# A hybrid encoder block: the first MLP product turned token-major, two of its eight K pairs by a seven-product scheme

## The chip, the cores and the metric

The kernel runs on one core of one Trainium2 chip. The metric is the device time of one execution in microseconds, as the median of the runs. The engines are called PE (TensorE), ACT (ScalarE), DVE (VectorE), POOL (GpSimd) and SP (SyncE, which here only issues DMA transfers). Each works through its own row of instructions in order.

## The reference

One layer over 256 tokens of width 2048, all in float32:

```python
n = rms_norm(h, norm_mix_w)                 # h = x
y = token_mixer(n @ w_in)                   # 8 gated DeltaNet heads, 8 HGRN2 heads, chunked recurrences
h = h + y @ w_out                           # 2048 x 2048
n = rms_norm(h, norm_ffn_w)
h = h + square(relu(n @ w_ff1)) @ w_ff2     # 2048 -> 8192 -> 2048
out = rms_norm(h, norm_final_w)
```

The change concerns `n @ w_ff1`: 256 tokens, K = 2048, 8192 columns out.

## The kernel before

Every large product is done as three products of float32r numbers. `split` (L111) makes them: ACT casts a block to float32r (`hi`, L117), DVE subtracts that from the block (`lo`, L118), and the product is hi*hi + hi*lo + lo*hi, summed in PSUM. Weights come in tiles of 1 MB (`wtile`, 128 x 2048, three buffers, loaded on SP's queue), and each is split in two halves of 128 x 1024, into a pool `spool` of three pairs of buffers. The activations are split once and stay in SBUF.

The stages, in the order of the program:

1. The input projection (L270 to L295) and the head mixers. Projections of the next head are issued among the mixing of the one before. The last two HGRN2 heads (`hgrn_mix`, L518 to L619) are long chains of small steps on DVE, ACT, POOL and PE: gates (L527 to L543), a scan (L547), decay factors `E` (L553 to L569), small matmuls `pd` and `pa` (L583 to L598), a masked sum (L601 to L608), copies (L611 to L615), the output `poh` (L617, L618) and `finish_heads` (L386): a square, its split, two matmuls `pm` (L398, L399), the scaling, and at last the split of the head's output into `yTb` (L117, L118). All tiles of the mixer lie in the pool `mp`, which is closed after the last head (`mctx.close()`, L636).
2. W_out (L652 to L671), two halves of 1024 columns, 192 matmuls each; then h is added, squared and summed, and 16 blocks of h are transposed on PE (L678) and split into `hT` (`to_T`), with the norm's weight; its row scale is applied at the very end, since the squared ReLU lets it pass.
3. The first MLP product (L698 to L715), feature-major: the weight block of 128 x 128 is stationary and the tokens move. For each K block and each of four blocks of features there are two matmuls: L709 with `hi` against both parts of the tokens (512 columns) and L710 with `lo` against the high part (256). After K, ACT copies and DVE adds the two halves of the bank, and DVE makes the squared ReLU. The result `g` is already as the second product needs it.
4. The second MLP product (L735 to L756), token-major: `gs`, the split of a block of g, is stationary, and the weights move, 512 columns at a time, three matmuls for each bank (L731).
5. The last norm and the output.

PSUM has four banks `acc` (psA) and, once the mixer is closed, four banks `accb` (psB).

The instructions are not put in the order in which the code is written: a scheduler lays out each engine's row when the program is built, so W_out's matmuls stand among those of the last heads. A tile of a pool that takes over the memory of a closed pool waits until the old pool's instructions are done.

Of the kernel before, what the change touches and what calls it, by code (L numbers as in the profile page):

```python
# [7 lines left out]
F32 = mybir.dt.float32  # L8
F32R = mybir.dt.float32r
AF = mybir.ActivationFunctionType  # L10
ALU = mybir.AluOpType
# [4 lines left out]
P = 128  # L16
T = 256
D = 2048
KT = D // P
DFF = 8192  # L20
NH = 8
CH = 64
EPS = 1e-6
LEVELS = (32, 16, 8, 4, 2)
NL = len(LEVELS)
NM = NL + 1
# [47 lines left out]
def hybrid_block(ctx: ExitStack, tc: tile.TileContext, x, xt, w_in, w_ab, params, w_out, w_ff1, w_ff2,  # L74
                 norm_final_w, consts, out):
    nc = tc.nc
    PE, ACT, DVE, POOL, SP = nc.tensor, nc.scalar, nc.vector, nc.gpsimd, nc.sync
# [11 lines left out]
    psA = ctx.enter_context(tc.tile_pool(name="psA", bufs=4, space=PSUM))  # L89

    yctx = ExitStack()
    ypool = yctx.enter_context(tc.tile_pool(name="ypool", bufs=1))
    NYA = 12
    yTa = ypool.tile([P, NYA, 2 * T], F32R, tag="yT", name="yTa")
# [7 lines left out]
    def acc_a():  # L102
        return psA.tile([P, 512], F32, tag="acc", name="acc")
# [19 lines left out]
        return hi, lo  # L123


    big = bpool.tile([P, 2 * D], F32, tag="h", name="big")
    x3 = big.rearrange("p (k t) -> p k t", k=KT)
    cst = cpool.tile([P, consts.shape[1]], F32, tag="cst", name="cst")
# [12 lines left out]
    for a, b in zip(xs, ws):  # L141
        SP.dma_start(*a)
        SP.dma_start(*b)
    SP.dma_start(cst, consts)
    wab = mp.tile([P, KT, 16], F32, tag="Xt", name="wab")
    SP.dma_start(wab, w_ab)

    def C(name):
        a, b = _CONST_COLS[name]
        return cst[:, a:b]  # L150

    ident, ones = C("ident"), C("ones")
    eps = C("eps")
# [487 lines left out]
    def acc_b():  # L641
        return psB.tile([P, 512], F32, tag="accb", name="accb")

    hT = bpool.tile([P, KT, 2 * T], F32R, tag="xT", name="hT")
    h = bpool.tile([P, 2 * D], F32, tag="h", name="h").rearrange("p (f c) -> p f c", f=2)
# [5 lines left out]
    fs = cpool.tile([P, 16], F32, tag="fs", name="fs")  # L651
    for nh in range(2):  # L652
        accs = [acc_a() for _ in range(4)]
        for kp in range(8):
            w = wtile()
            SP.dma_start(w, w_out[nh * 8 + kp])
            for kk in range(2):
                k = 2 * kp + kk
                hi, lo = split(w[:, kk * 1024:(kk + 1) * 1024], 1024)
                for hf in range(2):  # L660
                    for a, ww in ((0, hi), (T, hi), (0, lo)):
                        st = yT(k, a + hf * P, a + hf * P + P)
                        for c in range(2):
                            PE.matmul(accs[2 * hf + c], lhsT=st, rhs=ww[:, c * 512:(c + 1) * 512],  # L664
                                      start=(k == 0 and a == 0 and ww is hi), stop=(k == 2 * NH - 1 and ww is lo))
        for hf in range(2):
            for c in range(2):
                hv = h[:, hf, nh * 1024 + c * 512:nh * 1024 + (c + 1) * 512]
                DVE.tensor_tensor(out=hv, in0=accs[2 * hf + c], in1=hv, op=ALU.add)
            hv = h[:, hf, nh * 1024:(nh + 1) * 1024]  # L670
            ACT.activation(sqj, hv, AF.Square, accum_out=fs[:, 2 * hf + nh:2 * hf + nh + 1])  # L671
        for k2 in range(4):
            pt = acc_b()
            for kk in range(2):
                k = nh * 8 + k2 * 2 + kk
                ptk = pt[:, kk * T:(kk + 1) * T]
                for hf in range(2):
                    PE.transpose(ptk[:, hf * P:(hf + 1) * P], h[:, hf, k * P:(k + 1) * P], ident)  # L678
                to_T(hT, k, ptk, cols[:, 16 + k:17 + k])
    for hf in range(2):  # L680
        DVE.tensor_tensor(out=fs[:, 4 + hf:5 + hf], in0=fs[:, 2 * hf:2 * hf + 1], in1=fs[:, 2 * hf + 1:2 * hf + 2],
                          op=ALU.add)
    DVE.tensor_scalar(fs[:, 4:6], fs[:, 4:6], 1.0 / D, EPS, ALU.mult, ALU.add)
    DVE.reciprocal(fs[:, 6:8], fs[:, 4:6])
    octx.close()
    yctx.close()


    fp = ctx.enter_context(tc.tile_pool(name="fp", bufs=1))
    NF = DFF // P  # L690
    NG = NF // 2
    gt = [fp.tile([P, NG, T], F32, tag=f"g{i}", name=f"g{i}") for i in range(2)]

    def g(f):
        return gt[f // NG][:, f % NG, :]

    nfw = fp.tile([P, D], F32, tag="nfw", name="nfw")
    for fg in range(NF // 4):  # L698
        accs = [acc_a() if fg % 2 == 0 else acc_b() for _ in range(4)]
        for kq in range(4):  # L700
            w = wtile()
            SP.dma_start(w, w_ff1[fg * 4 + kq])
            for q in range(2):
                hi, lo = split(w[:, q * 1024:(q + 1) * 1024], 1024)
                for kk in range(2):
                    k = 4 * kq + 2 * q + kk
                    for f in range(4):
                        cs = slice(kk * 512 + f * P, kk * 512 + (f + 1) * P)
                        PE.matmul(accs[f], lhsT=hi[:, cs], rhs=hT[:, k, :], start=(k == 0), stop=False)  # L709
                        PE.matmul(accs[f][:, T:], lhsT=lo[:, cs], rhs=hT[:, k, 0:T], start=False, stop=(k == KT - 1))  # L710
# [7 lines left out]
    accs = [[acc_a() for _ in range(4)], [acc_b() for _ in range(4)]]  # L718
    TAIL = 3
    held = []  # L720

# [10 lines left out]
                      start=(first and a == 0 and ww is hi), stop=(last and ww is lo))  # L732

    keep = None
    for f in range(NF):  # L735
        w = wtile()
        SP.dma_start(w, w_ff2[f])
        gs = fp.tile([P, 2 * T], F32R, tag="gs", name="gs", bufs=4)
        split(g(f), None, gs[:, 0:T], gs[:, T:])
        n = f - (NF - TAIL)  # L740
        if n == 0:
            keep = fp.tile([P, TAIL - 1, 2, D], F32R, tag="g0", name="keep")
        hl = []
        for q in range(2):
            qs = slice(q * 1024, (q + 1) * 1024)
            if 0 <= n < TAIL - 1:
                hl.append(split(w[:, qs], None, keep[:, n, 0, qs], keep[:, n, 1, qs]))
            else:
                hl.append(split(w[:, qs], 1024))
# [7 lines left out]
    fin = fp.tile([P, 12], F32, tag="fin", name="fin")  # L757
    sqf = fp.tile([P, 512], F32, tag="sqf", name="sqf")
    o = fp.tile([P, 2, D], F32, tag="o", name="o", bufs=1)
    NP = 5  # L760
    DVE.memset(fin, 0.0)

    def piece(hf, n, a, b, acc):
        hv = h[:, hf, a:b]
        DVE.scalar_tensor_tensor(out=hv, in0=acc, scalar=fs[:, 6 + hf:7 + hf], in1=hv, op0=ALU.mult, op1=ALU.add)
        ACT.activation(sqf[:, 0:b - a], hv, AF.Square, accum_out=fin[:, hf * NP + n:hf * NP + n + 1])
        DVE.scalar_tensor_tensor(out=o[:, hf, a:b], in0=hv, scalar=float(D) ** 0.5, in1=nfw[:, a:b], op0=ALU.mult,
                                 op1=ALU.mult)

    def row_rstd(hf, n, last):  # L770
# [11 lines left out]

    def scaled(hf, eng, a, b, s):
        if eng is ACT:
            ACT.activation(h[:, hf, a:b], o[:, hf, a:b], AF.Copy, scale=s)
        else:
            DVE.tensor_scalar(h[:, hf, a:b], o[:, hf, a:b], s, None, ALU.mult)
        (ACT if eng is ACT else SP).dma_start(out[0, hf * P:(hf + 1) * P, a:b], h[:, hf, a:b])

    hv = h[:, 1, 1536:2048]  # L790
# [10 lines left out]
            ff2(f, 1, c, gs, hl)  # L801
        piece(1, c, c * 512, (c + 1) * 512, accs[1][c])
    for n in range(2):
        bank = acc_a()[:, 0:256]
# [13 lines left out]
def _laid_out(i):  # L818
# [5 lines left out]
    for base in (0, 4112):  # L824
        v = w[:, base:base + 4096].reshape(2, 8, P, 2, 2, NH, P)
        groups.append(v.transpose(5, 3, 0, 2, 1, 4, 6).reshape(4 * NH, P, 2048))

    def columns(a):
        return a.reshape(-1, P).T

# [9 lines left out]
        "w_ff1": i["w_ff1"][0].reshape(4, 4, P, 16, 512).transpose(3, 0, 2, 1, 4).reshape(64, P, 2048),  # L840
# [24 lines left out]
```

## Time and profile before

| | us |
|---|---|
| median of three runs | 1272.61 (1271.04 to 1273.03) |
| the profiled execution | 1271.04 |
| its span, from the first instruction to the last | 1269.3 |
| PE busy (matmuls) | 1239.6 |
| DVE, ACT, POOL busy | 855.0, 673.9, 166.3 |
| mean granted clock of TensorE | 0.994 of full |

A row of the profile's timeline gives the start, the duration, the engine, the line of the kernel, the operation, output<-inputs, the shape, and how many instructions are merged in the row; in brackets stands how long the engine had been idle and what released it. Matmuls overlap one another: the distance between two starts tells the pace, not the duration. In a row of a table by stretches of time there are, after the stretch and its length, the busy time of PE, PE's weight loads, DVE, ACT and POOL, each with the number of instructions, then the granted clock, the share of DMA and GB/s. In a group row the numbers are count | busy us, mean ns of one | idle time before.

### The profile page before, as it was taken

To read this page: it belongs to the slowest core of one execution; us is meant where nothing else is said; L and a number is where in the kernel's file an instruction comes from. 1 tells how busy PE (TensorE), PEld (TensorE's weight loads), DVE (VectorE), ACT (ScalarE), POOL (GpSimd) and SP (SyncE) were. 2 spreads that over 40 slices of the span, in tenths; PEclk is the share of its full clock that TensorE was granted. 3 is DMA by queue.
4 is the path that set the end of the run, shared out by engine and by line. 5 is a ranking of instruction groups with operands and counts; after the bars stand their busy time and mean duration, and the time that the engine had idled before them with its cause. 6 is when DMAs were issued, how large, how long until landed. Compare 5 with 4: busy or idle time off the path is not lost.

```text
span 1269.3 us, 18524 instructions
## 1 busy us (share of the span) xinstructions
PE 1239.6 (98%) x7293; PEld 1050.3 (83%) x7293; DVE 855.0 (67%) x1211; ACT 673.9 (53%) x973; POOL 166.3 (13%) x216
## 2 busy tenths in 40 slices
PE   7999999998999999999999999999999999999997
PEld 5888888876788887888888888888888888888886
DVE  7789999889988996566555565555655545545556
ACT  7567677655667775455444444444444444444453
POOL 1233433278300130000000000000000000000000
PEclk9999999998999999999999999999999999999999
DMA  8455555533434544465555545555455555555552
GB/s 314 147 176 172 179 186 187 173 141 133 151 104 174 189 167 166 168 222 177 197 181 184 199 170 195 189 178 196 168 201 195 199 199 190 187 191 195 199 201 97
DMA packets 35798, 229.65 MB, mean 181 GB/s; under 512 B 4536, under 2 KB 5440, under 8 KB 8960
## 3 DMA queue, kind: packets, MB, share of 16 engines
q1 hardware_dynamic: 33408, 225.63, 50.4%
q0 software_dynamic: 1728, 2.11, 1.3%
q8 instruction: 57, 0.93, 0.3%
q10 hardware_dynamic: 576, 0.74, 0.2%
q14 instruction: 29, 0.24, 0.1%
HBM read 225.83 MB, written 2.63 MB: 180 GB/s over the span
## 4 chain that ended last, share of the span: by engine, by line
issue 62%; PE 30%; POOL 3%; DVE 2%; DMA 2%; ACT 0%; SPq 0%; POOLq 0%; ACTq 0%; DVEq 0%
PE acc L286 15%; PE acc L287 8%; PE acc L664 3%; POOL Xt L424 1%; POOL X L426 1%; DMA big<-in_xt_dram 1%; DMA w<-in_w_in_dram 1%; DVE E L568 1%; PE pk L368 1%; DVE E L553 0%; DVE lo L118 0%; PE pd L583 0%; PE pab L221 0%; PE po L507 0%; PE pk L369 0%
## 5 line engine op out<-in xcount | busy, mean ns | idle before, releaser
L118 DVE TENSOR_TENSOR lo<-w,hi 128x1024 fp32r<-128x1024 f32 (+1 forms) x416 | 517.3, 1244 | 363.5 <-ACT hi L117 362.4
L117 ACT CAST hi<-w 128x1024 fp32r<-128x1024 f32 (+1 forms) x416 | 433.2, 1042 | 442.0 <-PE accb L731 177.1
L286 PE MATMUL acc<-xT,hi 128*128 128x512 f32 x1024 | 363.3, 401 | 7.1 <-ACT hi L117 6.7
L287 PE MATMUL acc<-xT,lo 128*128 128x256 f32 x1024 | 283.9, 286 | 6.2 <-DVE lo L118 6.2
L286 PEld LDWEIGHTS acc<-xT,hi 128*128 128x128 f32 x1024 | 191.6, 191 | 47.3 <-ACT hi L117 7.3
L287 PEld LDWEIGHTS acc<-xT,lo 128*128 128x128 f32 x1024 | 194.9, 191 | 15.0 <-DVE lo L118 10.5
L709 PE MATMUL acc<-hT,hi 128*128 128x512 f32 x512 | 181.3, 399 | 0.0
L709 PE MATMUL accb<-hT,hi 128*128 128x512 f32 x512 | 180.8, 398 | 0.0
L731 PE MATMUL accb<-hi,gs 128*128 128x512 f32 x494 | 170.0, 389 | 0.0
L710 PE MATMUL accb<-hT,lo 128*128 128x256 f32 x512 | 143.2, 281 | 0.0
L710 PE MATMUL acc<-hT,lo 128*128 128x256 f32 x512 | 142.8, 281 | 0.0
L731 PE MATMUL acc<-hi,gs 128*128 128x512 f32 (+1 forms) x500 | 134.2, 388 | 0.0
L709 PEld LDWEIGHTS accb<-hT,hi 128*128 128x128 f32 x512 | 96.1, 188 | 23.9
L709 PEld LDWEIGHTS acc<-hT,hi 128*128 128x128 f32 x512 | 96.0, 188 | 23.4
L731 PEld LDWEIGHTS acc<-hi,gs 128*128 128x128 f32 x500 | 93.7, 188 | 19.3
L731 PEld LDWEIGHTS accb<-hi,gs 128*128 128x128 f32 x494 | 92.7, 188 | 19.3
L779 POOL TENSOR_TENSOR fin<-fin,cst 128x1 f32<-128x1 f32 x2 | 1.1, 564 | 773.9 <-issue 766.5
L710 PEld LDWEIGHTS acc<-hT,lo 128*128 128x128 f32 x512 | 96.5, 189 | 0.2
L710 PEld LDWEIGHTS accb<-hT,lo 128*128 128x128 f32 x512 | 96.6, 189 | 0.1
L731 PE MATMUL accb<-lo,gs 128*128 128x512 f32 x247 | 95.4, 389 | 0.0
L731 PE MATMUL acc<-lo,gs 128*128 128x512 f32 (+1 forms) x250 | 77.7, 388 | 0.0
L731 PEld LDWEIGHTS acc<-lo,gs 128*128 128x128 f32 x250 | 46.9, 188 | 9.7
(251 smaller groups left out, 1250.1 us busy)
## 6 DMA issues: line engine op xcount, KB each, us to landing
w<-in_w_ff_dram SPq DMA_DIRECT2D x128, 1024.0 KB, 4.9
w<-in_w_in_dram SPq DMA_DIRECT2D x62, 1024.0 KB, 4.9
w<-in_w_out_dram SPq DMA_DIRECT2D x16, 1024.0 KB, 4.9
big<-in_xt_dram SPq DMA_DIRECT2D x8, 256.0 KB, 6.2
w<-in_w_in_dram SPq DMA_DIRECT2D x8, 256.0 KB, 6.3
h<-in_x_dram SPq DMA_DIRECT2D x2, 1024.0 KB, 9.2
dt<-scr_g POOLq DMA_DIRECT2D x8, 128.0 KB, 5.6
nfw<-in_norm_final_w_dram SPq DMA_DIRECT2D x1, 1024.0 KB, 4.7
```

The source lines that it names most:

```text
L117: ACT.copy(hi, w)
L118: eng.tensor_tensor(out=lo, in0=w, in1=hi.bitcast(F32), op=ALU.subtract)
L286: PE.matmul(accs[g], lhsT=hi[:, kk, g, :], rhs=xT[:, k, :], start=(k == 0), stop=False)
L287: PE.matmul(accs[g][:, T:], lhsT=lo[:, kk, g, :], rhs=xT[:, k, 0:T], start=False, stop=(k == KT - 1))
L368: PE.matmul(pk0, lhsT=R[:, 1, 0:P], rhs=qk.rearrange("p a t -> p (a t)"), start=True, stop=True)
L424: POOL.tensor_tensor(out=t3, in0=X[:, j, j + 1:].unsqueeze(2).to_broadcast([np_, nr, ncol]), in1=X[:, j, 0:ncol].unsqueeze(1).to_broadcast ...
L426: POOL.tensor_tensor(out=X[:, j + 1:, 0:ncol], in0=X[:, j + 1:, 0:ncol], in1=t3, op=ALU.subtract)
L568: DVE.tensor_tensor(out=ev, in0=ev, in1=view(gx, 0, [[2 * m, nb], [T + m, 2], [1, m]]), op=ALU.mult)
L664: PE.matmul(accs[2 * hf + c], lhsT=st, rhs=ww[:, c * 512:(c + 1) * 512], start=(k == 0 and a == 0 and ww is hi), stop=(k == 2 * NH - 1 and ...
L709: PE.matmul(accs[f], lhsT=hi[:, cs], rhs=hT[:, k, :], start=(k == 0), stop=False)
L710: PE.matmul(accs[f][:, T:], lhsT=lo[:, cs], rhs=hT[:, k, 0:T], start=False, stop=(k == KT - 1))
L731: PE.matmul(dst, lhsT=gs[:, a + hf * P:a + hf * P + P], rhs=ww[:, at:at + n], start=(first and a == 0 and ww is hi), stop=(last and ww is lo))
```

## The change

*The first product becomes token-major*, as the second is: a block of 128 tokens (high or low part) is stationary, and 512 columns of weights move (`product`, three matmuls). The 8192 columns are done in 8 groups (`ng`) of 1024, two blocks of 512; four banks E hold the two token halves by the two column blocks. K goes in 8 pairs (`kp`) of two blocks of 128. Six pairs are plain: 24 matmuls each.

*Pairs 2 and 5 (`SUMS`) use the Strassen-Winograd scheme*: seven products of sums of token blocks with sums of weight blocks, in place of eight, 21 matmuls. The token sums are formed and split once (`blocks`, `a_sums`). The weight sums are formed on DVE for each tile (`TT`: one difference of 1024 columns, two of 512), and three pairs and a half of hi and lo are split in place of two. Four of the products go to four more banks M; after pair 5 they are combined into `C4` (a copy on ACT, four additions on DVE), and at the end of the group the E banks are added to that (four additions on DVE) and ACT applies the ReLU. E and M are the banks acc and accb by turns.

*The result is token-major and has to be turned*: `turn` transposes four blocks of 128 x 128 on PE and ACT squares the bank into g. The turns of a group are kept in a list, `fills`, and issued two at a time in the next group, so their banks are E's of the group before. The 16 transposes of h go into the same list for the second half.

*Buffers.* A second pool of split buffers, `wp2`, has two pairs; `split_pair` takes pairs 1, 2 and 5 of each five from `spool` and pairs 3 and 4 from `wp2`, from W_out on. `wp2` and `tp` (`TT`, a half pair and the second set of token sums) are opened at the right end of SBUF after the mixer is closed. h is written to DRAM in four pieces of 512 KB and loaded back (with the final norm's weight) after the first product, on SP's queue. The constants that only the mixer needs move into `mp`. The first two blocks of the second product do their first 1024 columns ahead of their second.

The core of the diff:

```diff
+    wp2 = ctx.enter_context(tc.tile_pool(name="wp2", bufs=2, side="right"))
+    t1 = ExitStack()
+    tp = t1.enter_context(tc.tile_pool(name="tp", bufs=1, side="right"))
+    pairs = [0]
+    def split_pair(w):
+        n = pairs[0] = pairs[0] + 1
+        pool, t = (spool, "") if n % 5 < 3 else (wp2, "2")
+        return split(w, None, *[pool.tile([P, 1024], F32R, tag=p + t, name=p + t) for p in ("hi", "lo")])
...
     for nh in range(2):
-        accs = [acc_a() for _ in range(4)]
+        acc = (acc_a, acc_b)[nh]
+        accs = [acc() for _ in range(4)]
...
-                hi, lo = split(w[:, kk * 1024:(kk + 1) * 1024], 1024)
+                hi, lo = split_pair(w[:, kk * 1024:(kk + 1) * 1024])
...
+            SP.dma_start(scr_h[hf, :, nh * 1024:(nh + 1) * 1024], hv)
...
+    def product(dst, a, b, start, stop):
+        (ah, al), (bh, bl) = a, b
+        PE.matmul(dst, lhsT=ah, rhs=bh, start=start, stop=False)
+        PE.matmul(dst, lhsT=al, rhs=bh, start=False, stop=False)
+        PE.matmul(dst, lhsT=ah, rhs=bl, start=False, stop=stop)
+    def turn(ng, n, src, acc):
+        half, hf = n // 2, n % 2
+        pt = acc()
+        for c in range(4):
+            PE.transpose(pt[:, c * P:(c + 1) * P], src[:, c * P:(c + 1) * P], ident)
+        ACT.activation(g(8 * ng + 4 * half, 4)[:, :, hf * P:(hf + 1) * P], pt.rearrange("p (c t) -> p c t", c=4),
+                       AF.Square)
...
-                    for f in range(4):
-                        cs = slice(kk * 512 + f * P, kk * 512 + (f + 1) * P)
-                        PE.matmul(accs[f], lhsT=hi[:, cs], rhs=hT[:, k, :], start=(k == 0), stop=False)
-                        PE.matmul(accs[f][:, T:], lhsT=lo[:, cs], rhs=hT[:, k, 0:T], start=False, stop=(k == KT - 1))
-        for f in range(4):
-            lot = fp.tile([P, T], F32, tag="lotf", name="lotf", bufs=2)
-            ACT.copy(lot, accs[f][:, T:])
-            DVE.tensor_tensor(out=lot, in0=accs[f][:, 0:T], in1=lot, op=ALU.add)
-            DVE.scalar_tensor_tensor(out=g(4 * fg + f), in0=lot, scalar=0.0, in1=lot, op0=ALU.max, op1=ALU.mult)
+    for ng in range(NGR):
+        bank_e, bank_m = (acc_a, acc_b) if ng % 2 == 0 else (acc_b, acc_a)
+        E = [bank_e() for _ in range(4)]
+        M = None
+        for kp in range(KP):
+            w = wtile()
+            SP.dma_start(w, w_ff1[ng * KP + kp])
+            if kp not in SUMS:
+                B12, B11 = halves(split_pair(w[:, 0:1024]))
+                B21, B22 = halves(split_pair(w[:, 1024:2048]))
+                plain_quad(E, a_plain(kp), ((B11, B12), (B21, B22)), kp == 0, kp == KP - 1, 0 if kp == 0 else 2)
+                if kp == 0:
+                    fill(2)
...
+            for dst, a, b in ((E[0], 1, B21), (E[1], 6, B22), (p5, 3, B1), (p7, 5, B3), (p6, 4, B2), (E[2], 2, B4),
+                              (p1, 0, B11)):
+                m = a in (0, 3, 4, 5)
+                product(dst, A[a], b, a0 and m, z0 and m)
...
+        for at, p in ((0, E[0]), (2, E[1]), (1, E[2]), (3, E[3])):
+            DVE.tensor_tensor(out=C4[:, at], in0=p, in1=C4[:, at], op=ALU.add)
+            ACT.activation(C4[:, at], C4[:, at], AF.Relu)
+            fills.append(lambda ng=ng, at=at, src=C4[:, at], acc=bank_e: turn(ng, at, src, acc))
```

What the scheduler makes of it, at three places. Lines ahead of the change move by four (L399 becomes L403, L617 becomes L621), and W_out's matmul L664 becomes L726.

PE's row around the last HGRN2 head, before (`pvh` is that head's first matmul, `pd` and `pa` follow; `acc<-hi` and `acc<-lo` are W_out's):

```order
L664 MATMUL acc<-lo,yTa 128x512 x4
L664 MATMUL acc<-hi,yTa 128x512
L522 MATMUL pvh<-cst,R 128x128 x2
L664 MATMUL acc<-hi,yTa 128x512 x2
L583 MATMUL pd<-E 32x32 x32
L586 MATMUL pd<-gx 32x64 x8
L592 MATMUL pa<-E 32x32 x4
L596 MATMUL pa<-E 64x64 x2
L598 MATMUL pa<-L 128x128
L664 MATMUL acc<-hi,yTa 128x512
L664 MATMUL acc<-lo,yTa 128x512 x2
L664 MATMUL acc<-hi,yTa 128x512 x4
```

The same head in PE's row after the change, to its end:

```order
L526 MATMUL pvh<-cst,R 128x128 x2
L587 MATMUL pd<-E 32x32 x8
L596 MATMUL pa<-E 32x32 x4
L587 MATMUL pd<-E 32x32 x24
L590 MATMUL pd<-gx 32x64 x8
L600 MATMUL pa<-E 64x64 x2
L602 MATMUL pa<-L 128x128
L621 MATMUL poh<-A,vv 128x256
L622 MATMUL poh<-A,vv 128x128
L402 MATMUL pm<-shi,ones_r 128x256
L403 MATMUL pm<-slo,ones_r 128x256
L726 MATMUL acc<-hi_5066,yTa 128x512 x8
```

Of W_out's 384 matmuls, 180 stand ahead of the last head's L399 before, and 24 ahead of its L403 after. `hi_5066` is the third pair of W_out, the first from `wp2`.

ACT's row at the end of the same head, before:

```order
L117 CAST hi<-w 128x1024 x2
L392 ACTIVATE fsq<-poh 128x256
L396 CAST shi<-fsq 128x256
L117 CAST hi<-w 128x1024 x2
L400 ACTIVATE fsq<-pm,cst 128x256
L401 ACTIVATE fsq<-fsq 128x256
L117 CAST yTb<-fsq 128x256
L117 CAST hi<-w 128x1024
```

And after:

```order
L619 COPY A<-pa 32x2x32 x2
L396 ACTIVATE fsq<-poh 128x256
L400 CAST shi<-fsq 128x256
L404 ACTIVATE fsq<-pm,cst 128x256
L405 ACTIVATE fsq<-fsq 128x256
L119 CAST yTb<-fsq 128x256
L119 CAST hi_5066<-w 128x1024
L119 CAST hi_5082<-w 128x1024
```

The casts of W_out's weights that stood between the head's steps are gone from there, and the third and fourth pair (`hi_5066`, `hi_5082`) come behind its last cast.

DVE's row at the end of a group of the first product, before (four blocks of features) and after (1024 columns; `C` is C4, the four additions of L835 to L838 are those of the M banks):

```order
L118 TENSOR_TENSOR lo<-w,hi 128x1024 x7
L714 TENSOR_TENSOR lotf<-acc,lotf 128x256 x2
L715 SCALAR_TENSOR_TENSOR g_5658<-lotf 128x256 x2
L118 TENSOR_TENSOR lo<-w,hi 128x1024
L714 TENSOR_TENSOR lotf<-acc,lotf 128x256 x2
```

```order
L838 TENSOR_TENSOR C_7937<-accb,C_7937 128x512
L120 TENSOR_TENSOR lo<-w,hi 128x1024
L816 TENSOR_TENSOR TT<-w 128x1024
L120 TENSOR_TENSOR lo_8138<-w,hi_8137 128x512
L120 TENSOR_TENSOR lo<-w,hi 128x1024
L841 TENSOR_TENSOR C_7937<-acc,C_7937 128x512
L819 TENSOR_TENSOR TT<-w,TT 128x512
L841 TENSOR_TENSOR C_7937<-acc,C_7937 128x512 x2
L820 TENSOR_TENSOR TT<-w,TT 128x512
L841 TENSOR_TENSOR C_7937<-acc,C_7937 128x512
L120 TENSOR_TENSOR lo<-w,hi 128x1024
```

Ahead of the E additions (L841) stand a split and the first difference for the next group; the additions come among the next two differences (L819, L820), and more splits behind them.

More of the change, by code (lines that the diff above doesn't have):

```diff
@@ L23 @@
 EPS = 1e-6
+NKEEP = 130
 LEVELS = (32, 16, 8, 4, 2)
@@ L149, in C @@
         a, b = _CONST_COLS[name]
-        return cst[:, a:b]
+        return cst[:, a:b] if b <= NKEEP else cst_a[:, a - NKEEP:b - NKEEP]
     ident, ones = C("ident"), C("ones")
@@ L671, in hybrid_block @@
             ACT.activation(sqj, hv, AF.Square, accum_out=fs[:, 2 * hf + nh:2 * hf + nh + 1])
[L672 to L689, printed above, removed]
+            SP.dma_start(scr_h[hf, :, nh * 1024:(nh + 1) * 1024], hv)
+        for kp in range(nh * 4, nh * 4 + 4):
+            if nh == 0:
+                blocks(kp, acc)
+            else:
+                fills.append(lambda kp=kp: blocks(kp, acc_b))
     NF = DFF // P
     NG = NF // 2
-    gt = [fp.tile([P, NG, T], F32, tag=f"g{i}", name=f"g{i}") for i in range(2)]
@@ new lines, in hybrid_block, with columns @@
+    t1.close()
+    f2 = ctx.enter_context(tc.tile_pool(name="f2", bufs=1, side="right"))
+    tail = bpool.tile([P, 8192], F32, tag="xT", name="tail")
+    h, nfw, o0 = tail[:, 0:2 * D].rearrange("p (f c) -> p f c", f=2), tail[:, 2 * D:3 * D], tail[:, 3 * D:]
+    for hf in range(2):
+        SP.dma_start(h[:, hf, :], scr_h[hf])
+    SP.dma_start(nfw, norm_final_w.unsqueeze(0).to_broadcast([P, D]))
+    accs = [[None] * 4, [None] * 4]
+    def columns(q, bank):
+        for hf in range(2):
+            for c in (2 * q, 2 * q + 1):
+                accs[hf][c] = bank()
@@ L719, in hybrid_block @@
+    columns(0, bank_m)
     TAIL = 3
@@ L734, in hybrid_block @@
     keep = None
+    late = []
     for f in range(NF):
```

156 lines of the change are left out of this document (128 added, 28 removed).

## The prediction

> **What bounds the kernel now.** I read the busy table first, then the waits of PE, then PE's rows in order of time, and last the rows of DVE, ACT and POOL where the head mixers end. The busy table:
>
> ```profile
> PE 1239.6 (98%) x7293; PEld 1050.3 (83%) x7293; DVE 855.0 (67%) x1211; ACT 673.9 (53%) x973; POOL 166.3 (13%) x216
> ```
>
> PE is busy 98% of the 1269.3 us span, so time is made or lost only there: by what PE must issue, and by holes in its row. The rows around the first MLP product:
>
> ```profile
> 549.53 0.43 PE L678 MATMUL accb<-cst,h 128*128 128x128 f32 x2
> ...
> 750.15 0.40 PE L709 MATMUL acc<-hT,hi 128*128 128x512 f32 x1
> 750.39 0.28 PE L710 MATMUL acc<-hT,lo 128*128 128x256 f32 x1
> 750.51 0.40 PE L709 MATMUL acc<-hT,hi 128*128 128x512 f32 x1
> ...
> 912.69 0.62 PE L731 MATMUL acc<-hi,gs 128*128 128x512 f32 x2
> 916.78 1.07 PE L731 MATMUL acc<-hi,gs 128*128 128x512 f32 x4
> 917.69 1.07 PE L731 MATMUL accb<-hi,gs 128*128 128x512 f32 x4
> 918.60 0.62 PE L731 MATMUL acc<-lo,gs 128*128 128x512 f32 x2
> 919.05 0.62 PE L731 MATMUL accb<-lo,gs 128*128 128x512 f32 x2
> 919.50 0.61 PE L731 MATMUL accb<-hi,gs 128*128 128x512 f32 x2
> ```
>
> The first column is the start. The first MLP product runs from 549.53 to 912.69, 363.2 us; its pairs of a 512- and a 256-column matmul start every 0.35 us. The second MLP product issues only 512-column matmuls: 12 from 916.78 to 919.50, 226.7 ns each. That second pattern (token block stationary, weights moving, three matmuls to a product) is the one the first product takes over.
>
> The other place is where the last two mixer heads end:
>
> ```profile
> 454.76 0.28 PE L399 MATMUL pm<-slo,ones_r 128*128 128x256 f32 x1
> ...
> 460.51 0.42 DVE L527 SCALAR_TENSOR_TENSOR u<-R,u 128x256 f32<-128x256 f32 x1
> 463.78 1.22 DVE L118 TENSOR_TENSOR lo<-w,hi 128x1024 fp32r<-128x1024 f32 x1
> 466.79 1.42 DVE L118 TENSOR_TENSOR lo<-w,hi 128x1024 fp32r<-128x1024 f32 x1
> 476.86 1.76 DVE L568 TENSOR_TENSOR E<-E,gx 128x256 f32<-128x256 f32 x5
> 479.14 1.22 DVE L118 TENSOR_TENSOR lo<-w,hi 128x1024 fp32r<-128x1024 f32 x1
> 480.27 0.42 DVE L572 TENSOR_TENSOR L<-E,ec 128x256 f32<-128x256 f32 x1
> 485.26 0.73 PE L583 MATMUL pd<-E 128*32 128x32 f32 x62
> 488.56 0.41 ACT L615 COPY A<-pa 32x64 f32<-32x64 f32 x2
> 493.40 0.59 PE L617 MATMUL poh<-A,vv 128*128 128x256 f32 x2
> 495.10 0.43 DVE L397 TENSOR_TENSOR slo<-fsq,shi 128x256 fp32r<-128x256 f32 x1 [1.24 <-ACT shi L396]
> 498.08 0.28 PE L399 MATMUL pm<-slo,ones_r 128*128 128x256 f32 x1
> 501.27 0.42 DVE L118 TENSOR_TENSOR yTb<-fsq,yTb 128x256 fp32r<-128x256 f32 x1 [0.47 <-ACT yTb L117]
> 501.29 1.65 PE L664 MATMUL acc<-hi,yTb 128*128 128x512 f32 x6 [2.93 <-ACT yTb L117]
> ```
>
> Here the last head's chain passes between DVE, ACT, POOL and PE for 41 us, and PE has only one hole, 2.93 us: it fills the rest with W_out. By the order, 180 of W_out's 384 matmuls stand ahead of the last head's L399 and 204 behind it.
>
> **The change, part by part.**
>
> *W_out loses its place beside the mixer (slower).* In the changed order only 24 W_out matmuls stand ahead of the last head's L403 (the old L399) and 360 behind it. The third pair of W_out is the first of the new pool `wp2`; its cast stands on ACT behind the last head's `yTb`, and its matmuls on PE behind all of both heads. PE works in order, so from about 456 us it has only the heads' small matmuls. When does it resume? I follow the last head's chain and take out the time in which it stood behind W_out work: 1.3 us behind the split at 463.78, 1.3 at 466.79, 1.1 at 479.14, 4.6 from L572's end (480.69) to L583, 4.4 from the copy's end (488.97) to L617, 2.4 from slo's end (495.53) to the pm pair that ends at 498.36, some 0.8 in smaller pieces: 15.9 us. Two splits of later W_out pairs still stand ahead of its start on ACT and delay it by about 1 us; PE works on the other head less. So the chain ends at 501.69 - 15.9 + 1.0 = 486.8, by the bare durations some 0.8 earlier; I take 486. One cast of 1.05 us (below) later PE starts W_out again: 487.1. PE has then been nearly idle for 31 us, and what an idle stretch does to it is seen here:
>
> ```profile
> 298.00:300.00 2.00, 0.37 (x5) 0.23 (x5) 2.00 (x5) 0.00 (x0) 0.00 (x0) 0.56 0.21 37
> 300.00:302.00 2.00, 2.00 (x7) 1.81 (x8) 2.00 (x4) 0.27 (x1) 1.87 (x3) 0.50 0.77 262
> 302.00:304.00 2.00, 2.00 (x9) 1.71 (x8) 1.87 (x4) 1.81 (x3) 1.76 (x4) 0.50 0.57 234
> 304.00:306.00 2.00, 2.00 (x10) 1.72 (x10) 0.86 (x1) 0.82 (x1) 2.00 (x4) 0.73 0.25 37
> ```
>
> The granted clock (third from the right) is 0.50 for the first 4 us of dense work and 0.73 in the next 2: 2.5 us lost. Transposes are priced by these rows:
>
> ```profile
> 513.25 1.03 PE L678 MATMUL accb<-cst,h 128*128 128x128 f32 x8
> 514.04 1.87 PE L664 MATMUL acc<-hi,yTa 128*128 128x512 f32 x7
> 515.75 0.62 PE L664 MATMUL acc<-lo,yTa 128*128 128x512 f32 x2
> ```
>
> Eight take 0.79 us, and the seven matmuls behind them 1.71 where 7 x 0.2267 is 1.59: 0.91 us for eight. W_out ends at 487.1 + 360 x 0.2267 (81.6) + 16 transposes (1.8) + 2.5 = 573.0, against 549.53: **+23.5 us**. Bounds: a chain 4 us shorter or longer (its smaller gaps taken out, or its POOL and ACT steps as late as now), and 0 to 3 us of clock.
>
> *The first product (faster).* 2048 matmuls go, 1488 of 512 columns come (8 groups: six plain pairs of 24, two of 21). At 226.7 ns that is 337.3 us; without the seven-product form it would be 48 matmuls, 10.9 us, more. 14 turns of eight transposes: 12.7. The 16 transposes of h are there before and after: 1.8. Sum 351.8 against 363.2: **-11.4 us**. Two more turns fall into the second product: **+1.8**. Bounds: eight transposes cost at least 0.45 us (128 columns each, in proportion to 512 in 226.7 ns) and at most 1.7 (the pair at 549.53 took 0.43): -7 to +13 us over 16 turns; I take the x8 row, since a turn is such a run.
>
> *What hides the rest.* The durations:
>
> ```profile
> L118 DVE TENSOR_TENSOR lo<-w,hi 128x1024 fp32r<-128x1024 f32 x408 | 511.8, 1255 | 362.7 <-ACT hi L117 361.5 <-PE accb L678 0.6
> L117 ACT CAST hi<-w 128x1024 fp32r<-128x1024 f32 x408 | 428.4, 1051 | 442.0 <-PE accb L731 177.1 <-PE accb L709 95.2 <-PE acc L709 92.1
> L569 DVE TENSOR_TENSOR E<-E,gx 128x512 f32<-128x512 f32 x8 | 5.4, 679 | 0.0
> L669 DVE TENSOR_TENSOR h<-acc,h 128x512 f32<-128x512 f32 x8 | 5.0, 683 | 1.5 <-PE acc L664 1.5
> L544 ACT ACTIVATE u<-u 128x512 f32<-128x512 f32 x8 | 5.1, 633 | 5.2 <-DVE u L543 5.1
> w<-in_w_ff_dram SPq DMA_DIRECT2D x128, 1024.0 KB, 4.9
> ```
>
> A group is 43.9 us on PE (186 x 0.2267 + 1.8). DVE: 18 splits and 2 differences of 1255 ns, 6 halves of 679, 8 bank additions of 683 = 34.6 us. ACT: 18 casts of 1051, 11 ops of 633 = 25.9 us. Five pairs of split buffers let DVE run ahead; a pair with sums needs 7.0 us of DVE for 4.8 of PE, its plain neighbours 2.5 for 5.4. At a group's end DVE must add E[3] before it splits on, but kp0's two pairs and kp1's first stand ahead of those additions: 8 us of PE work, against 2 additions and one split, 2.6 us. The turns wait for ReLUs that are by then done. A 1 MB tile has 5.5 us and lands in 4.9, through the same three buffers. So I cost all this at nothing, with 0.5 us in the first group, whose blocks of h also pass through DVE; if the cover is gone, each group pays up to 2.6 us, 20.8 in all. On SP's queue the writes of h (4 x 512 KB), its return and the norm weights (3 MB, behind PE's last product) stand ahead of weight loads; the fifth tile of the second product is needed some 22 us after them, and at the 4.9 us per MB of the row they take 15: nothing, up to 3 us if they crowd.
>
> Sum: 23.5 - 11.4 + 1.8 + 0.5 = +14.4 us on the profiled execution's 1271.04 (its span of 1269.3 and 1.7 around it): 1285.4. The median of the runs, 1272.61, lies 1.57 above that execution: **1287**.
>
> Two rules of the Trainium skill would move this. "TensorE: Matmul & The Clock Gate", section "Back-to-back issue gap", gives N/2.4 + 2.5 ns for isolated warm matmuls, 216 ns at N = 512; by that the sum would be 16 us lower, and the trace does not agree (226.7). The same page, "Part 4: PE-mode transpose", states about 275 ns for a transpose in a kernel; by that 128 of them cost 35 us instead of 14.6, and the rows' 114 ns do not agree either.
>
> **Rivals.**
> - *Products issue faster than now, and it is no slower.* If a product's matmuls started every 217 ns, 1488 x 9.7 ns = 14.4 us would pay for the hole: 1272.6. For it: 512 columns are all there is to stream. Against: the same pattern stands at 226.7 at 916.78, with PE never waiting. This is the case in which the first rule above would hold.
> - *The hole closes early.* Break-even needs PE back on W_out at 472.7, 14.4 us sooner, from a chain that starts at about 461.5 and whose durations alone come to 20. Time 1273 or less.
> - *Group ends stall.* E's banks change roles; if additions, ReLUs and turns delay the next splits at every end, 20.8 us: 1308. Against: DVE has 9 us a group to spare.
> - *Transposes are dear* (1.7 us for eight): 1300. Against: the x8 row. The second rule above would give 1307.
> - *The order is not kept.* That W_out still fills the hole is excluded: PE and ACT take their rows in turn.
>
> **How the numbers follow.** Forecast as worked out 0.77; group ends stall 0.10; dear transposes 0.04; faster products 0.05; early end 0.04. The first three are slower (0.91); of the last two I put 0.05 on within 0.2% (2.5 us, about what a measurement of this kernel can tell) and 0.04 on faster. Low end: the chain 4 us shorter, no clock loss, cheap transposes by half: 1287 - 4 - 2.5 - 3.5 = 1277. High end: chain 4 us longer, 1 us a group: 1299, and I leave the rivals outside.
>
> **What would show it.** PE without W_out matmuls from about 456 to 487, then granted clock near 0.5 for some us; W_out's last matmul at 570 to 575 against 549.08; the first product 350 to 354 us long, with 227 ns between matmuls and no wait for `lo` over 1 us; turns of eight transposes in 0.9 us; second product and tail as before. Wrong would be: W_out rows inside the hole, PE waits at group starts, or products spaced other than 227 ns.

## The result, and the profile after

The changed kernel takes **1293.07 us** (median of four runs, 1292.58 to 1293.54) against 1272.81 us (1271.04 to 1273.03): a ratio of 1.0165, interval 1.015 to 1.018. It is slower, by 20.3 us where 14.4 was forecast. The profiled execution has a span of 1291.8 us against 1269.3. That gap is 2.2 us larger than the medians', because the execution of before lies 1.77 us below its median and the one of after 0.47 above.

The busy table of the page:

```profile
PE 1246.8 (97%) x6861; PEld 1035.6 (80%) x6861; DVE 918.4 (71%) x1233; ACT 716.1 (55%) x1015; POOL 165.1 (13%) x216
```

PE is still the bound. Its rows in order of time, from the last head to the end of the second product:

```profile
457.53 0.40 PE L726 MATMUL acc<-lo,yTa 128*128 128x512 f32 x1
457.77 0.38 PE L526 MATMUL pvh<-cst,R 128*128 128x128 f32 x2
...
482.56 0.58 PE L403 MATMUL pm<-slo,ones_r 128*128 128x256 f32 x1
487.05 3.78 PE L726 MATMUL acc<-hi,yTa 128*128 128x512 f32 x8 [3.90 <-ACT hi L119]
490.63 1.77 PE L726 MATMUL acc<-lo,yTa 128*128 128x512 f32 x4
492.24 1.99 PE L726 MATMUL acc<-hi,yTa 128*128 128x512 f32 x8
...
573.09 0.62 PE L726 MATMUL accb<-lo,yTb 128*128 128x512 f32 x2
573.55 0.40 PE L752 MATMUL acc<-hi,sets 128*128 128x512 f32 x1
...
929.33 0.39 PE L754 MATMUL accb<-lo,sets 128*128 128x512 f32 x1
929.56 0.62 PE L872 MATMUL acc<-hi,gs 128*128 128x512 f32 x2
...
932.28 1.03 PE L764 MATMUL accb<-cst,C 128*128 128x128 f32 x8
933.08 0.71 PE L872 MATMUL acc<-hi,gs 128*128 128x512 f32 x2
933.62 0.40 PE L872 MATMUL acc<-lo,gs 128*128 128x512 f32 x1
...
1266.17 0.63 PE L872 MATMUL acc<-keep,gs 128*128 128x512 f32 x2
```

The wait at 487.05 is for ACT. DVE's row shows the first and the last step of the last head's chain, and ACT's shows that W_out's cast is released by that last step:

```profile
462.02 0.41 DVE L531 SCALAR_TENSOR_TENSOR u<-R,u 128x256 f32<-128x256 f32 x1
...
485.49 0.42 DVE L120 TENSOR_TENSOR yTb<-fsq,yTb 128x256 fp32r<-128x256 f32 x1 [0.47 <-ACT yTb L119]
```

```profile
485.95 1.99 ACT L119 CAST hi<-w 128x1024 fp32r<-128x1024 f32 x2 [0.49 <-DVE yTb L120]
```

From 457.5 to 487.05 PE has no W_out matmul. The granted clock (third from the right) then stays at 0.50 through some 5 us of dense work:

```profile
476.00:486.00 10.00, 4.47 (x28) 2.94 (x20) 3.60 (x8) 2.96 (x10) 0.76 (x2) 0.50 0.01 2
488.00:490.00 2.00, 2.00 (x6) 1.54 (x5) 1.45 (x2) 0.00 (x0) 0.00 (x0) 0.50 0.00 0
490.00:492.00 2.00, 2.00 (x6) 1.51 (x6) 0.00 (x0) 1.05 (x1) 0.00 (x0) 0.50 0.77 193
492.00:494.00 2.00, 2.00 (x10) 1.67 (x9) 1.23 (x1) 0.00 (x0) 0.00 (x0) 0.97 0.79 332
```

Stage by stage, from these rows and those of before:

| stage | before, us | after, us | difference | forecast |
|---|---|---|---|---|
| start to first product | 549.5 | 573.6 | +24.0 | +23.5 |
| first product | 363.2 | 356.0 | -7.2 | -11.4, +0.5 |
| second product, to the first kept weight (`keep`) | 331.8 | 336.6 | +4.8 | +1.8 |
| from there to the end | 24.8 | 25.6 | +0.9 | 0 |
| span | 1269.3 | 1291.8 | +22.5 | +14.4 |

So the hole came as forecast, and 8.1 us more were lost, 6.7 of them in the two MLP products (3.7 and 3.0). PE doesn't wait there: the profile lists no wait of PE behind 488 us. Nor is it the clock, which was granted in full in both, as it was in both products of before (1.00 from 549 to 913 and from 913 to 1244 us):

```profile
573.00:930.00 357.00, 357.00 (x1622) 293.46 (x1621) 265.27 (x291) 199.25 (x243) 0.00 (x0) 1.00 0.53 191
930.00:1266.00 336.00, 336.00 (x1479) 275.92 (x1478) 173.20 (x186) 151.31 (x190) 0.00 (x0) 1.00 0.57 198
```

The matmuls start further apart. These are the first rows of six runs of 12 matmuls in the second product; each run reads one pair of split buffers:

```profile
1000.01 0.61 PE L872 MATMUL accb<-hi,gs 128*128 128x512 f32 x2
...
1002.73 0.63 PE L872 MATMUL acc<-hi,gs 128*128 128x512 f32 x2
...
1005.49 0.62 PE L872 MATMUL accb<-hi,gs 128*128 128x512 f32 x2
...
1008.24 0.63 PE L872 MATMUL acc<-hi,gs 128*128 128x512 f32 x2
...
1011.01 0.61 PE L872 MATMUL accb<-hi,gs 128*128 128x512 f32 x2
...
1013.73 0.61 PE L872 MATMUL acc<-hi,gs 128*128 128x512 f32 x2
```

The runs take 2.72, 2.76, 2.75, 2.77 and 2.72 us: 226.7 ns a matmul at both ends, and 229 to 231 between. This repeats every five runs, as the five pairs of split buffers do. Over all rows, gaps over 260 ns left out (they stand right behind a turn), the mean is 228.7 ns in the second product and 229.8 in the first; in the second product of before it was 226.7 throughout. Of each five runs, counted from the product's start, the second and third read the new pairs (`wp2`), and the fourth reads the old pair that comes after them.

### The profile page after: what moved, and what is told of

It reads as the page before. It is cut to its first block, busy times and chain, and to the rows that moved or that the text cites. A ratio compares the mean times of both kernels' runs of the same rounds, so it can differ in the third digit from the quotient of the medians.

```text
span 1291.8 us, 17738 instructions
## 1 busy us (share of the span) xinstructions
PE 1246.8 (97%) x6861; PEld 1035.6 (80%) x6861; DVE 918.4 (71%) x1233; ACT 716.1 (55%) x1015; POOL 165.1 (13%) x216
## 4 chain that ended last, share of the span: by engine, by line
PE 61%; issue 1%; ACT 0%; DVE 0%; POOLq 0%; POOL 0%
PE acc L872 13%; PE accb L872 13%; PE accb L752 4%; PE acc L752 4%; PE acc L754 4%; PE accb L754 4%; PE acc L753 4%; PE accb L753 4%; PE accb L726 3%; PE acc L726 3%; PE accb L764 1%; PE acc L764 1%; PE acc L696 0%; PE accb L696 0%; PE poh L621 0%
## 5 line engine op out<-in xcount | busy, mean ns | idle before, releaser
L120 DVE TENSOR_TENSOR lo<-w,hi 128x1024 fp32r<-128x1024 f32 (+1 forms) x416 | 506.4, 1223 | 270.2 <-ACT hi L119 265.1
L119 ACT CAST hi<-w 128x1024 fp32r<-128x1024 f32 (+1 forms) x416 | 424.3, 1024 | 371.5 <-PE accb L872 96.5
L872 PE MATMUL acc<-hi,gs 128*128 128x512 f32 (+1 forms) x500 | 154.8, 391 | 0.0
L872 PE MATMUL accb<-hi,gs 128*128 128x512 f32 x494 | 152.7, 391 | 0.0
L752 PE MATMUL accb<-hi,sets 128*128 128x512 f32 x248 | 98.2, 396 | 0.0
L752 PE MATMUL acc<-hi,sets 128*128 128x512 f32 x248 | 98.2, 396 | 0.0
L872 PE MATMUL acc<-lo,gs 128*128 128x512 f32 (+1 forms) x250 | 97.6, 390 | 0.0
L754 PE MATMUL accb<-lo,sets 128*128 128x512 f32 x248 | 97.3, 392 | 0.0
L754 PE MATMUL acc<-lo,sets 128*128 128x512 f32 x248 | 97.0, 393 | 0.0
L753 PE MATMUL acc<-hi,sets 128*128 128x512 f32 x248 | 96.9, 391 | 0.0
L753 PE MATMUL accb<-hi,sets 128*128 128x512 f32 x248 | 96.8, 391 | 0.0
L120 DVE TENSOR_TENSOR lo<-TT,hi 128x1024 fp32r<-128x1024 f32 x32 | 39.2, 1225 | 38.9 <-ACT hi L119 36.9
L119 ACT CAST hi<-TT 128x1024 fp32r<-128x1024 f32 x32 | 33.4, 1045 | 40.6 <-PE acc L753 13.9
```

The costliest lines, as they stand in the source:

```text
L119: ACT.copy(hi, w)
L120: eng.tensor_tensor(out=lo, in0=w, in1=hi.bitcast(F32), op=ALU.subtract)
L752: PE.matmul(dst, lhsT=ah, rhs=bh, start=start, stop=False)
L753: PE.matmul(dst, lhsT=al, rhs=bh, start=False, stop=False)
L754: PE.matmul(dst, lhsT=ah, rhs=bl, start=False, stop=stop)
L872: PE.matmul(dst, lhsT=gs[:, a + hf * P:a + hf * P + P], rhs=ww[:, at:at + n], start=(first and a == 0 and ww is hi), stop=(last and ww is lo))
```

## Experiments

Two things were to be shown: that the hole comes from the new buffers alone, and what widens the matmuls. Times are medians beside the kernel before on the same chip (1272.6 to 1272.8).

**W_out from the old buffers.** The changed kernel with

```
-                hi, lo = split_pair(w[:, kk * 1024:(kk + 1) * 1024])
+                hi, lo = split(w[:, kk * 1024:(kk + 1) * 1024], 1024)
```

and with `pairs = [32]` in place of `[0]`, so that the later pairs alternate as they did.

> The changed kernel, but W_out's split pairs all come from the three old buffers; the first and second MLP product keep the five pairs. Theory A (the lost overlap comes from the new buffers, which lie in memory that the mixer still holds, and from nothing else): PE fills the last head's chain with W_out again, W_out's last matmul ends near 549.5 us instead of 573.5, and the time falls by 23 to 24 us to 1269 to 1270. Rival (the last heads hold W_out back for another reason too, as their own rows in the order or the residual in its new pool): W_out's end stays above 560 and the time above 1280. Both leave the two MLP products as in the changed kernel, 356 and 336.6 us up to the first kept weight.

Measured: 1270.34 us, 22.7 less than the changed kernel; against before 0.9982 (0.9972 to 0.9991). PE runs W_out through the last head again:

```profile
460.39 1.43 PE L726 MATMUL acc<-hi,yTa 128*128 128x512 f32 x5
...
548.45 0.62 PE L726 MATMUL accb<-lo,yTb 128*128 128x512 f32 x2
```

**Only that in the kernel before:** two of five pairs of W_out from a new pool over the mixer's memory, nothing else of the change.

> The kernel before, with one thing of the change alone: two of every five pairs of W_out's split buffers come from a new pool opened where the mixer's memory was. Theory A: this alone costs what the changed kernel lost there, 23 to 24 us: 1296 to 1297, with W_out's end near 573.5, PE without W_out from about 458 to 487, and the first product still 363 us long behind it. Rival (the loss needs the other moves of the change): 1280 or less. Where the pairs lie in another place than the old ones W_out's own matmuls may be spaced 2 to 3 ns wider, up to 1 us in all.

Measured: 1294.25 us, 21.5 more than before (1.0171, 1.0156 to 1.0186), and the same hole:

```profile
457.20 0.38 PE L522 MATMUL pvh<-cst,R 128*128 128x128 f32 x2
...
486.50 3.78 PE L674 MATMUL acc<-hi,yTa 128*128 128x512 f32 x8 [3.90 <-ACT hi L117]
...
572.28 0.61 PE L674 MATMUL acc<-lo,yTb 128*128 128x512 f32 x2
```

W_out's last row moved from 549.08 by 23.2 us. With the first kernel this shows the cause from both sides: it is enough to put the new pairs there, and taking them away gives it back. The time came 2 us under the expectation, which counted in spans: these differ by 23.2 us (1292.5 against 1269.3), the medians by 21.5.

**gs in another pool.** `gs = f2.tile(...)` becomes `gs = fp.tile(...)`.

> The changed kernel, with the small tile gs (the stationary operand of the second product) in the pool of g instead of the one at the right end of the memory, where the new pairs lie. In the changed kernel the second product's matmuls start every 228.7 ns in the mean, 226.7 for two of every five pairs of buffers and 229 to 231 for the other three; before it was 226.7 throughout. Theory B1 (the stationary and the moving operand slow each other where gs lies beside the new pairs): back to 226.7, the second product 3 us shorter, time 1290. Theory B2 (the new pairs' place alone, or the old pairs' new place, or when the buffers are written): spacing as in the changed kernel, time 1293.

Measured: 1293.18 us, second product 336.6 us as in the changed kernel. B1 falls: the neighbourhood is not it. By the addresses of the built program gs begins at 160 modulo 256 bytes in both places, so this run leaves open whether its place modulo 256 counts; later ones show that it does.

**Second product from the old buffers only** (`split` for `split_pair` there).

> The changed kernel, with the second product's splits in the three old buffers only. Theories B1 and B2 with the new pairs as the cause: 226.7 ns throughout the second product, 3 us shorter, time 1290. Theory B3 (the old buffers lie elsewhere than before, and that is the cause): spacing of 228 to 231 ns stays. Theory B4 (with three pairs ACT and DVE write less far ahead, and PE waits): PE shows waits for hi or lo in the second product and the time is above 1293.

Measured: 1289.62 us, 3.5 less; its second product 333.7 us at 226.7 ns. Here the first rows of runs are 2.72 us apart each time:

```profile
1000.95 1.29 PE L872 MATMUL acc<-hi,gs 128*128 128x512 f32 x5
...
1003.67 1.29 PE L872 MATMUL accb<-hi,gs 128*128 128x512 f32 x5
...
1006.39 1.29 PE L872 MATMUL acc<-hi,gs 128*128 128x512 f32 x5
```

So the new pairs are in it; B3 (the old pairs' place by itself) and B4 fall. But the kernel before with the new pool reads new pairs at the very same addresses (their `hi` at 212960 and 217056 in each partition, by the built programs) and shows no widening in W_out: behind 505 us its matmuls start every 227.1 ns, against 227.0 in the kernel before and 228.5 in the changed one. What differs is the old pairs' place: in the changed kernel `cst` is 4944 bytes shorter, and all pools behind it lie 4928 bytes lower, so the old pairs begin at 160 modulo 256 and the new ones at 224, where both began at 224 in that kernel. That gave the next theory.

**64 bytes ahead of the new pairs.**

```
+    padp = ctx.enter_context(tc.tile_pool(name="padp", bufs=1, side="right"))
+    padp.tile([P, 16], F32, tag="pad", name="pad")
     wp2 = ctx.enter_context(tc.tile_pool(name="wp2", bufs=2, side="right"))
```

> The changed kernel, with a tile of 64 bytes a partition laid out ahead of the new pairs, which moves them (and the tiles beside them) by 64 bytes and changes nothing else. In the changed kernel the three old pairs begin at 32 modulo 128 bytes and the two new ones at 96; matmuls start every 226.7 ns only while PE reads an old pair and ACT and DVE write an old pair, and every 229 to 231 ns where a new one is read or written. With the same new pairs at the same addresses, but the old ones at 96 too, W_out was at 226.7 throughout. Theory C (operands and results whose places differ by 64 bytes modulo 128 slow each other): with all pairs at 32 the spacing is 226.7 in W_out, the first and the second product, which end 0.9, 4.7 and 3.0 us shorter: time 1284 to 1285. Rival D (the distance or the region of memory matters, not the 64 bytes): nothing changes, 1293.

Measured: 1288.32 us, 3 to 4 above the expectation. The first product went from 356.0 to 351.7 us, 226.9 ns between matmuls:

```profile
573.37 0.39 PE L754 MATMUL acc<-hi,sets 128*128 128x512 f32 x1
...
925.05 0.62 PE L874 MATMUL acc<-hi,gs 128*128 128x512 f32 x2
```

The second stayed at 336.9: the same 64 bytes had moved `gs`, and now all five pairs ran at 228.9 ns alike. The expectation had overlooked that. With W_out's old buffers as well:

> Both at once: W_out's pairs from the three old buffers, and the 64 bytes ahead of the new pairs. Theory A with C: 1270.3 less 7.7 us (4.7 in the first product, 3.0 in the second): 1262 to 1263, faster than both kernels. Rival D: 1270.

Measured: 1265.50 us (0.9946, 0.9931 to 0.9961), above the expected 1262 to 1263 for the same reason: theory C held for the first product, and the second again stayed at 336.9 us.

**The stationary operand moved in the kernel before:** 64 bytes between the split buffers and all that lies behind them.

> The kernel before, with 64 bytes laid out between the split buffers and everything behind them: the weights' tiles and the split pairs stay at 96 modulo 128, the stationary operands (xT, yT, hT as the moving one of the first product, gs) go to 32. Theory C1 (every operand that PE reads counts, the stationary one too): the second product's matmuls start every 229 to 231 ns instead of 226.7 and it takes 3 to 6 us longer; with the other stages the time is 1278 to 1285. Theory C2 (only the moving operand and what ACT and DVE write meanwhile count): the second product and W_out as before, 331.8 us; only the first product, where hT is the moving operand, may widen, by up to 3 ns for 1024 pairs. Rival D: 1272.8.

Measured: 1284.90 us, 12.1 slower for 64 unused bytes (1.010, 1.0085 to 1.0115). Its second product takes 341.6 us; the runs of 12 are now 2.80 us apart, 233.3 ns a matmul:

```profile
1001.91 1.10 PE L733 MATMUL acc<-hi,gs 128*128 128x512 f32 x4
...
1004.71 1.10 PE L733 MATMUL acc<-hi,gs 128*128 128x512 f32 x4
...
1007.51 1.10 PE L733 MATMUL acc<-hi,gs 128*128 128x512 f32 x4
```

C1 in kind, and more in size than expected (9.8 us in the second product, against 3 to 6); W_out's matmuls start every 233.3 ns too. The first product, whose moving operand is hT, did not widen (363.3 us from its first matmul, 363.0 before).

**One buffer after the other moved in the kernel before** (each split buffer 1040 elements long, 1024 used).

> The kernel before, with 64 bytes more in each of the three split buffers, of which only the first 1024 elements are used: hi and lo of a pair and neighbouring pairs then begin at 96 and 32 modulo 128 in turn. Theory C: the second product's 1464 matmuls start every 229 to 231 ns, it takes 3 to 6 us longer, and with W_out and the projections the time is 1277 to 1285. Rival D (distance or region): no change, 1272.8.

Measured: 1279.48 us (1.0056, 1.0039 to 1.0073), second product 339.9 us at 232.2 ns: in kind as theory C has it, and 8.1 us longer where 3 to 6 were expected. But the first product got 3.4 us shorter (359.6), which no theory here expected; that the time still fell into the expected range is luck. The longer buffers also move what lies behind them, by 384 bytes: gs goes to 96 modulo 256.

**Everything at one place:** old buffers for W_out, the 64 bytes, and gs in the pool of g.

> W_out's pairs from the old buffers, 64 bytes ahead of the new pairs, and gs in the pool of g, where it begins at 32 modulo 128 like every pair (with the 64 bytes alone it had gone to 96, and the second product stayed at 228.9 ns for all five pairs alike, where e3 with gs at 32 and the new pairs at 96 changed nothing). Theory C1 (stationary, moving and written operands together): 226.7 ns in the first and in the second product, the second 3.2 us shorter, time 1262 to 1263. Theory C2 (the stationary operand doesn't count): 1265.5, as without this move.

Measured: **1263.03 us**, 0.9928 of before (0.9913 to 0.9943), faster than both kernels. First and second product at 226.9 and 226.7 ns, the second 333.7 us:

```profile
999.73 0.61 PE L874 MATMUL accb<-hi,gs 128*128 128x512 f32 x2
...
1002.45 0.61 PE L874 MATMUL acc<-hi,gs 128*128 128x512 f32 x2
...
1005.17 0.61 PE L874 MATMUL accb<-hi,gs 128*128 128x512 f32 x2
```

**A control with 128 bytes** in place of 64, and gs in its own pool at the right end, which the 128 bytes move too.

> A control: W_out's pairs from the old buffers, and 128 bytes instead of 64 ahead of the new pairs, so that they stay at 96 modulo 128 while every address on that side moves. Theory C: as with no bytes there, 1270 us, 229.8 ns in the first product and 228.7 in the second. Rival (any move of that side changes the spacing): 1265 or another time.

Measured: 1273.36 us, 230.3 ns in the first product and 231.1 in the second. Theory C as I had written it, modulo 128, fails: a distance of 128 is not harmless. That shows where PE reads an old pair and old pairs are written, so that only gs lies elsewhere (32 against 160): these runs of 12 take 226.7 ns a matmul in the changed kernel and 232.6 here.

```profile
987.13 0.63 PE L874 MATMUL accb<-hi,gs 128*128 128x512 f32 x2
...
989.93 0.62 PE L874 MATMUL acc<-hi,gs 128*128 128x512 f32 x2
...
992.72 0.62 PE L874 MATMUL accb<-hi,gs 128*128 128x512 f32 x2
```

Modulo 256 the theory fits every one of these second products (where each tile begins, modulo 256 bytes, by the built programs):

| kernel | old pairs | new pairs | gs | ns between matmuls |
|---|---|---|---|---|
| before | 224 | none | 224 | 226.7 |
| after | 160 | 224 | 160 | 228.7 |
| gs in another pool | 160 | 224 | 160 | 228.7 |
| old buffers only | 160 | none | 160 | 226.7 |
| 64 bytes | 160 | 160 | 96 | 228.9 |
| everything at one place | 160 | 160 | 160 | 226.7 |
| 128 bytes | 160 | 96 | 32 | 231.1 |
| before, stationary moved | 224 | none | 32 | 233.3 |
| before, one after the other | 224, 32, 96 (hi); 160, 224, 32 (lo) | none | 96 | 232.2 |

The size follows a pattern as well. Where the pairs read and written lie at one place, the spacing goes with how far gs lies ahead of them modulo 256: 226.7 ns at 0, 233.3 at 64 (before, stationary moved), 232.6 at 128 (the runs above), 228.9 to 229.0 at 192 (64 bytes; the third of each five runs in the changed kernel and in the control). Other tiles moved with gs in some of these, so this is a pattern, not a cause shown.

The writes count too. In the changed kernel's fourth run of five, from 1008.24, PE reads gs and an old pair, both at 160, and yet it takes 230.9 ns a matmul. ACT begins to write a pair as the run before ends:

```profile
1008.21 1.05 ACT L119 CAST hi<-w 128x1024 fp32r<-128x1024 f32 x1 [1.70 <-PE accb L872]
```

The five pairs go in turn, so this cast fills the buffer that the third run read, a new one at 224. In the fifth and first run, where old pairs are read and written, it is 226.7. The profile doesn't name the buffer of each row; that it is this one is worked out from their order.

**What the seven-product form and the turns are worth**, in the kernel with everything at one place. First all K pairs plain:

> The kernel with everything at one place (W_out's pairs from the old buffers, 64 bytes, gs moved), without the seven-product form: all eight K pairs plain, 1536 matmuls in the first product instead of 1488, no differences on DVE and no additions of banks. If the first product is bound by what PE issues, as the prediction has it, it gets 48 x 226.7 ns = 10.9 us longer: 1273. If the seven-product form costs PE waits elsewhere, which go with it, less: below 1270.

Measured: 1273.60 us, 10.6 more. Then without the turns' transposes (in both kernels the rest is as in the one with everything at one place):

> The same kernel with everything at one place, without the 128 transposes of the turns: the squares are taken from the untransposed tile, so the values that go into the second product are not the reference's. The prediction's price of 0.91 us for eight transposes: 16 x 0.91 = 14.6 us less, 1247.5 to 1248.5. If transposes are dear (1.7 us for eight): 27 us less, 1235. If they fill gaps: 8 us less or still smaller, 1254 or above.

Measured: 1247.87 us, 15.2 less. The first product runs here, from its first row behind W_out to the second's first row, 362.3 us without the form and 338.9 without the transposes, against 351.5 (551.23 to 902.70):

```profile
549.36 0.39 PE L755 MATMUL acc<-hi,sets 128*128 128x512 f32 x1
...
911.69 0.62 PE L874 MATMUL acc<-hi,gs 128*128 128x512 f32 x2
```

```profile
549.00 0.39 PE L755 MATMUL acc<-hi,sets 128*128 128x512 f32 x1
...
887.88 0.62 PE L871 MATMUL acc<-hi,gs 128*128 128x512 f32 x2
```

## Why the prediction was right, and what it missed

- **W_out's hole, right in place and size.** PE back at 487.05 (forecast 487.1), the first product's start at 573.55 (573.0; W_out's own matmuls at 228.5 ns make up the difference). Taking the chain's delays out one by one gave the right end, closer than its parts were: the chain began 1.5 us later than before (1.0 forecast) and lasted 23.9 us, from 462.02 to 485.91, where 25.3 were left, 24.5 by the bare durations. That the end agrees to 0.1 us is partly luck. The 2.5 us of clock held: the first 8 matmuls took 447 ns and the next 4 403, 2.5 us above 226.7 each. The Trainium skill's "TensorE: Matmul & The Clock Gate", Part 1, "What's actually happening", has the clock at half until a window of about 3.4 us was busy; here it was at half for some 5 us, so the trace agrees in kind and took longer.
- **The first product, right in kind and 3.7 us too short.** The mis-sized term is 1488 x 226.7 ns: in this kernel they start every 229.8 ns, 4.6 us more; the 0.5 us for the first group did not show. Counts and all other prices held: with operands at one place the first product took 351.7 us, where 351.8 was the sum; the 48 matmuls that the form saves were worth 10.6 us (10.9 forecast); 128 transposes 15.2 (14.6).
- **The second product, 3.0 us too short,** is the same term: 1464 matmuls at 228.7 instead of 226.7 ns. "Second product as before" rested on the same lines of code; their operands had moved.
- **What hides the rest, right.** PE waits in neither product: the last wait that the profile lists for it is the one at 487.05. Of the 0.9 us at the end, 0.25 lies between the first kept weight and the last matmul (16.56 us, 16.31 before) and goes with the addresses: it is back at 16.31 with everything at one place. The other 0.6 lies behind the last matmul, 9.0 to 9.1 us in every changed kernel against 8.5, and stays unexplained.
- **Rivals.** Faster products: the opposite happened. The hole closing early: no. Group-end stalls: none. Dear transposes: the eight at 932.28 take 0.80 us, and 0.09 more of the pair behind them. The 114 ns at which the prediction put one transpose is a distance between starts. One transpose by itself lasts 0.27 us in these traces (270 to 273 ns in all 128 of the turns), so the row says nothing against a figure for that duration; what a run of them costs PE is the distance, and the sum stood.
- **The range held by luck.** 1293.07 lies 6 us above 1287 and inside 1277 to 1299, because the range had room for a chain 4 us longer and for stalls of 1 us a group. Neither came. What filled the room, the operands' places, had no term and no allowance.

The warning that products spaced other than 227 ns would make the forecast wrong named the right place. Its cause, where the tiles lie, was in none of the rivals: the prediction took the duration of an instruction as fixed by its shape.

## What to carry to other kernels

Opening a pool over memory that an earlier stage still holds delays the first user of it until that stage ends; if its work was to fill that stage's gaps, give it buffers that are free then, and open the pool for what comes later. When tiles move, even by a shortened constant in another pool, compare the start-to-start time of matmuls stage by stage: a change of 1% there, with no wait in the profile, is worth a look at the addresses. A duration read from the kernel before holds for the kernel after only with its operands laid out alike.

## What the runs showed that was not expected

In rows of 512-column matmuls alone, each with its own weight load, one started every 226.7 ns in the second products (226.9 in the changed first product, 227 in W_out) where the split pairs that PE reads and ACT and DVE write meanwhile and PE's stationary tile begin at the same place modulo 256 bytes in a partition, and every 228.5 to 233.3 ns, as the mean of a stage, where they don't; 64 bytes of padding moved the time by -4.8 us (the changed kernel and its version with W_out's old buffers) and by +12.1 us (the kernel before). The Trainium skill's "SBUF — State Buffer", section "SBUF: two separate sides", states that PE, ACT and DVE's dedicated ports never wait on anyone; no run here looks at ports, but a PE rate that depends on where tiles lie, those that other engines write among them, is not what it leads one to expect, and the measurement decides. Open remain the mechanism; whether 256 is the true period, since a distance of 256 was seen once only (W_out with the new pool in the kernel before: pairs at 224 and 480 modulo 512, 227.1 ns); and why the first product of the kernel before, with pairs of 512 and 256 columns, did not widen when hT moved by 64 bytes and gained 3.4 us from a mixed layout.
